# One hybrid decoder layer on Trainium2: attention row maxima passed by a 0/1 matmul, GpSimd scalings a step later, and two norms computed in another place

## The chip, the core and the metric

The kernel runs on one core of a Trainium2 chip: TensorE (PE) multiplies matrices, VectorE (DVE), ScalarE (ACT) and GpSimd (POOL) work on tiles of 128 partitions, SyncE (SP) and the other queues issue DMAs between HBM and SBUF. The metric is the time of one execution in device microseconds; the median of three runs of the kernel before is 1704.49 us (1704.07 to 1704.84).

## What is computed

One step of a decoder layer for a prompt of 512 tokens and 8 samples of 4 tokens each, 544 tokens in all, model width 1024:

```
x += 0.5 * SwiGLU_1(rms(x))                              # width 2816
h  = rms(x); qa, ka, va, qkv_b, z, b, a, gate = split(h @ w_in)
o_a = merge over 3 groups (window, dilation) = (128,1), (512,4), (2048,16)
      of softmax(q k / sqrt(128) - alibi) v              # 4 heads x 128 in each group
o_b = gated DeltaNet: conv of width 4, 8 heads, chunked exact solve, head norm, silu(z)
x += (sig(gA) * (o_a @ w_proj_a) + sig(gB) * (o_b @ w_proj_b)) @ w_out
x += 0.5 * SwiGLU_2(rms(x));   y = rms(x)

def _rms(x, w):  y = x * rsqrt(mean(x * x, -1) + 1e-6);  return y * w
def _merge_groups(outs, lses):  w = softmax(stack(lses), 0);  return sum(w[..., None] * stack(outs), 0)
```

It also returns the new rows of the caches, the convolution states and the DeltaNet states.

## The kernel before

Activations lie transposed, 128 features on the partitions and the 544 tokens as columns, in eight tiles x of 128x544; the columns are worked in two halves of 272 (NH). Weights come from HBM as f32 chunks (raw) and are split into a rounded part and a rest (G): ScalarE copies the rounded part, VectorE or GpSimd subtracts it (`split_next`, line 426). The activations are split in the same way (xh and xl, hh and hl, oh and ol). A unit is one tile of 128 matrix columns for one half: for each of its 128x128 weight tiles three matmuls, hi by xh, hi by xl and lo by xh, into one PSUM bank (`unit`, line 609), and an evacuation by VectorE or ScalarE. All engine instructions are recorded at one helper line, L122, so rows are told apart by their tiles.

`kernel_units` (line 677) walks through all units in a fixed order: feed-forward 1, the mixer, feed-forward 2. Everything else in the mixer is side work in Python generators: `attn_slot` (line 1459, four slots, one for each head of a group), `attn_sample`, `gdn_pair` (line 1056, four pairs of heads), the sample part of the DeltaNet, convolutions, z, `fin_a` (line 854, which brings the slots' outputs into the projection's input). Between two triples of matmuls `pump` (line 643) lets those generators take a step that are ready by the counted costs of the class `Meter` (line 48). Where something must have happened first (a convolution buffer free, SBUF tiles reserved), `until` (line 292) calls `force`, which steps the side work in order of its due time with no unit matmul between, until the condition holds. So the order on TensorE is set when the program is built.

SyncE's queue works in order: an instruction that waits holds up all loads behind it. In `attn_slot` the scores of a slot lie with tokens on the partitions in two layouts (positions of group 0, and of groups 1 and 2); to merge the groups, each layout needs the row maxima of the other (tile ast, X in the code). They are written to a DRAM scratch (md) and read back permuted, two writes and two reads a slot on SyncE's queue. A slot's output o goes to DRAM (oad) and `fin_a` reads it back.

In `gdn_pair` GpSimd scales v and k (tiles vk and kn) of both heads; VectorE makes the decay rows R, ScalarE exponentiates them; then TensorE makes the products of keys and queries (kq), and VectorE scales these into B and A. Later a chain of small steps (X, Pm, Y, Q, called lev in the code) inverts the block matrix: TensorE, then VectorE or ScalarE, then TensorE again.

At the start `build` (line 471) issues eight warm-up passes (WARM=4 f32 matmuls on zeros), splits half 0 of x, adds up the squares of half 0 on GpSimd (`norm_acc`, acc), splits half 1 and adds up its squares; `norm_fin` for half 0 comes after four units: a matmul with ones sums over the partitions, then nine VectorE operations on 128x272 make 1/rms. At the end the same happens for the last half, and `store_y` multiplies its eight tiles by it, two of them on GpSimd, and stores them.

Of the kernel before, what the change touches and what calls it, by code (L numbers as in the profile page):

```python
# [10 lines left out]
F32 = mybir.dt.float32  # L11
# [27 lines left out]

CFG = dict(S=62, S2=4, G=4, G2=8, RAW=2, U3=3, H=10, HM=6, LA=4, LAG=3.0, SLACK=0.0, BANKS=3, PRE=3, LOV=("pa", "pb", "ba", "z", "gate", "gdn", "at"), CV=0, WARM=4, EP=8, DUE=2, RES=0, RQ="gpsimd")  # L40

# [164 lines left out]
def consts():  # L206
# [54 lines left out]
class Builder:  # L261
# [214 lines left out]
    def build(self):  # L476
        nc, A = self.nc, self.A
        self.x = [self.S(name="x") for _ in range(KT)]
        vec = self.C([P, A["in_vec_dram"].shape[1]], name="vec")
        mats = self.C([P, A["in_mats_dram"].shape[1]], name="mats")  # L480
        warm = self.H()
# [19 lines left out]
        for k, n in enumerate(names):  # L501
            setattr(self, n, mats[:, k * P:(k + 1) * P])
        o = len(names) * P
        self.hb, self.mb, self.mh, self.cs = (mats[:, o:o + 32], mats[:, o + 32:o + 40],
                                              mats[:, o + 40:o + 44], mats[:, o + 44:o + 47])
        self.wn = [vec[:, k * 8:(k + 1) * 8] for k in range(4)]
# [3 lines left out]
        self.acc, self.r = [None, None], [None, None]  # L510
# [23 lines left out]
    def norm_acc(self, n, h):  # L534
        s = self.sl(h)
        if n == 0:
            self.acc[h] = [self.S([P, NH], name="acc")]
            self.act(self.acc[h][0], self.x[n][:, s], AF.Square)
        else:
            q = self.H()  # L540
            self.act(q, self.x[n][:, s], AF.Square)
            if self.last and n == KT - 1 and h == 1:
                self.acc[h].append(q)
            else:
                self.tt(self.acc[h][0], self.acc[h][0], q, ALU.add, self.nc.gpsimd)
        if self.last:
            self.act(self.x[n][:, s], self.x[n][:, s], AF.Copy, scale=self.wn[3][:, n:n + 1])
# [32 lines left out]
    def norm_fin(self, h):  # L580

        ps = self.mm_ps()[:, :NH]
        acc = self.acc[h]
# [14 lines left out]
        if h == 1:  # L598
            self.norm_no += 1

    def store_y(self, h):
        s = self.sl(h)
        for n in range(KT):
            f = self.H()
            self.tt(f, self.x[n][:, s], self.R(h), ALU.mult, self.nc.gpsimd if n % 3 == 2 else None)
            (self.nc.scalar if n % 2 and h else self.nc.sync).dma_start(self.A["out_y"][:, n, s], f)
# [70 lines left out]
    def kernel_units(self):  # L677
# [176 lines left out]
    def fin_a(self):  # L854
# [4 lines left out]
        for j in range(4):  # L859
            yield from self.need(3, True)  # L860
            t = self.S([P, NPR], name="oA")
            self.dma(t, self.oad[j])
            yield t
            hl = (self.S(dt=F32R, name="oh"), self.S(dt=F32R, name="ol"))
# [191 lines left out]
    def gdn_pair(self, h0):  # L1056
# [402 lines left out]
    def attn_slot(self, j):  # L1459
# [63 lines left out]
        lay = [lambda a: a.rearrange("s (a p) -> p (s a)", p=P), lambda a: a.rearrange("s (n r) -> n s r", r=4)]  # L1523
        fl = lambda a, i: a.rearrange("p s a -> p (s a)") if i == 0 else a
# [4 lines left out]
        yield X  # L1529
        yield "vector"  # L1530
# [312 lines left out]
```

## Time and profile before

| | us |
|---|---|
| median of three runs | 1704.49 |
| profiled execution | 1707.67 |
| its span, first to last instruction | 1705.8 |
| TensorE busy | 1646.0 (96%) |
| VectorE busy | 1012.1 (59%) |
| ScalarE busy | 620.8 (36%) |
| GpSimd busy | 165.5 (10%) |

The granted TensorE clock is 0.984 in the mean over the span (1 is 2.4 GHz, the upper of its two levels). Busy shares are averages over stages with different limits: feed-forward 1 runs from about 46 to 420 us, the mixer to about 1130, feed-forward 2 to about 1690, and the stages differ in how much of TensorE they use.

### The profile page before, as it was taken

How to read it: one execution, taken by the hardware profiler on the slowest of the kernel's cores; microseconds unless marked ns; L12 is line 12 of the kernel's file. 1: busy time of each engine (PE TensorE's matmuls, PEld its weight loads, DVE VectorE, ACT ScalarE, POOL GpSimd, SP SyncE). 2: the span in 40 equal slices, each digit the busy share in tenths (PEclk: the TensorE clock that was granted, in tenths of full speed). 3: DMA queues.
4: the chain of work that ended last, by engine and by line, in shares of the span. 5: the costliest groups of instructions: out<-in, count | busy, mean ns of one | idle time of the engine just before them, and what ended most of it. 6: DMA issues, size and time to landing. Idle time of an engine off the chain costs nothing.

```text
span 1705.8 us, 33626 instructions
## 1 busy us (share of the span) xinstructions
PE 1646.0 (96%) x13373; PEld 1604.1 (94%) x13373; DVE 1012.1 (59%) x2473; ACT 620.8 (36%) x1559; POOL 165.5 (10%) x289
## 2 busy tenths in 40 slices
PE   8999999999999999989999889899999999999997
PEld 7999999999898999988989779889999999999996
DVE  7754255545777978567785755353456654255534
ACT  5332223333453434445433345432333332232332
POOL 5000000011011211211121110000011000000012
PEclk9999999999999999999999989999999999999999
DMA  5222223221524454656666455432242323222221
GB/s 179 87 88 89 97 76 99 76 86 63 185 76 123 149 172 148 201 149 195 177 184 206 145 183 184 109 118 87 88 138 88 100 75 100 87 85 90 87 76 65
DMA packets 116434, 205.12 MB, mean 120 GB/s; under 512 B 30963, under 2 KB 57109, under 8 KB 116277
## 3 DMA queue, kind: packets, MB, share of 16 engines
q1 hardware_dynamic: 104708, 162.43, 30.4%
q0 software_dynamic: 10992, 39.99, 8.0%
q8 instruction: 105, 1.72, 0.4%
q10 hardware_dynamic: 576, 0.56, 0.1%
q14 instruction: 53, 0.43, 0.1%
HBM read 172.20 MB, written 30.73 MB: 119 GB/s over the span
## 4 chain that ended last, share of the span: by engine, by line
PE 81%; DVE 9%; DMA 5%; ACT 3%; issue 2%; SPq 1%; DVEq 0%; ACTq 0%
PE sd L122 42%; PE mm L122 39%; DMA md<-ast 3%; DVE H L122 1%; DVE G L122 1%; DVE inv L122 1%; DVE y L122 1%; ACT s L122 1%; SPq L122 1%; DMA ast<-md 1%; DVE Yc L122 1%; DVE R L122 1%; DVE nrm L122 1%; DVE xl L122 0%; ACT G L122 0%
## 5 line engine op out<-in xcount | busy, mean ns | idle before, releaser
L122 PE MATMUL mm<-xh,G 128*128 128x272 f32 x3632 | 743.7, 295 | 4.4 <-ACT G L122 2.0
L122 PEld LDWEIGHTS mm<-xh,G 128*128 128x128 f32 x3632 | 591.0, 191 | 18.2 <-issue 10.2
L122 PE MATMUL mm<-xl,G 128*128 128x272 f32 x1816 | 527.2, 290 | 0.4 <-DVE xl L122 0.4
L122 DVE TENSOR_TENSOR G<-raw,G 128x512 fp32r<-128x512 f32 x468 | 303.0, 689 | 169.9 <-ACT G L122 163.8
L122 PE MATMUL sd<-xh,G 128*128 128x272 f32 x1904 | 362.9, 288 | 0.0
L122 PEld LDWEIGHTS mm<-xl,G 128*128 128x128 f32 x1816 | 346.9, 191 | 1.8 <-DVE xl L122 0.6
L122 ACT ACTIVATE G<-raw 128x512 fp32r<-128x512 f32 x474 | 271.9, 622 | 105.4 <-PE mm L122 46.9
L122 PEld LDWEIGHTS sd<-xh,G 128*128 128x128 f32 x1904 | 300.0, 188 | 0.2
L122 PE MATMUL sd<-xl,G 128*128 128x272 f32 x952 | 273.6, 287 | 0.0
L122 PEld LDWEIGHTS sd<-xl,G 128*128 128x128 f32 x952 | 179.1, 188 | 0.1
L122 PE MATMUL sd<-hh,G 128*128 128x272 f32 x1287 | 163.1, 288 | 0.0
L122 PEld LDWEIGHTS sd<-hh,G 128*128 128x128 f32 x1287 | 161.9, 188 | 0.1
L122 POOL TENSOR_TENSOR acc<-acc,H 128x272 f32<-128x272 f32 x55 | 44.8, 815 | 917.6 <-ACT H L122 916.5
L122 ACT ACTIVATE hh<-H 128x272 fp32r<-128x272 f32 x88 | 38.0, 432 | 201.7 <-DVE H L122 201.7
L122 PE MATMUL mm<-hh,G 128*128 128x272 f32 x825 | 104.7, 288 | 0.0
L122 PEld LDWEIGHTS mm<-hh,G 128*128 128x128 f32 x825 | 103.8, 188 | 0.0
L122 ACT ACTIVATE H<-H 128x272 f32<-128x272 f32 (+1 forms) x89 | 38.2, 429 | 162.3 <-DVE H L122 162.3
L122 POOL DMA_DIRECT2D raw<-in_W_dram x76 | 41.5, 546 | 530.4 <-DVE G L122 280.7
L122 DVE SCALAR_TENSOR_TENSOR H<-H,H 128x272 f32<-128x272 f32 x120 | 54.5, 455 | 33.4 <-ACT H L122 32.8
L122 DVE SCALAR_TENSOR_TENSOR x<-sd,x 128x272 f32<-128x272 f32 x49 | 21.4, 438 | 78.2 <-PE sd L122 78.2
L122 DVE SCALAR_TENSOR_TENSOR y<-U,vec,y 128x568 f32<-128x568 f32 x72 | 61.1, 848 | 8.0 <-ACT y L122 5.1
L122 DVE TENSOR_TENSOR hh<-H,hh 128x272 fp32r<-128x272 f32 x88 | 38.9, 442 | 43.9 <-ACT hh L122 43.9
(262 smaller groups left out, 1772.4 us busy)
## 6 DMA issues: line engine op xcount, KB each, us to landing
raw<-in_W_dram SPq DMA_DIRECT2D x161, 512.0 KB, 3.5
raw<-in_W_dram POOLq DMA_DIRECT2D x76, 512.0 KB, 3.9
qkv<-qd SPq DMA_DIRECT2D x36, 256.0 KB, 3.8
st<-in_ssm_dram SPq DMA_DIRECT2D x32, 256.0 KB, 4.6
cache<-in_kc_dram SPq DMA_DIRECT2D x28, 256.0 KB, 4.6
cache<-in_vc_dram SPq DMA_DIRECT2D x28, 256.0 KB, 3.8
qd<-av SPq DMA_DIRECT2D x24, 256.0 KB, 2.7
out_dram<-av SPq DMA_DIRECT2D x24, 256.0 KB, 2.9
```

The lines of the kernel that those rows point to most:

```text
L122: r = f(*args, **kw)
```

## The change

Five things change.
1. `attn_slot`: the maxima go from one layout to the other by TensorE. Each layout's maxima are spread by a 0/1 mask over 32 columns, multiplied by a 0/1 matrix (by4 or its transpose of4, new columns of the constant tile mats), masked again and summed over four. The four DMAs through md go.
2. The last slot (j == 3) keeps its output in SBUF for `fin_a`.
3. `gdn_pair`: the four GpSimd scalings stand after each head's B and A step in place of before the R step.
4. The start: six warm-up matmuls, all first weight splits on VectorE (EP=0), the last two squares of half 0 handed to the norm's matmul in place of GpSimd's adds, `norm_fin(0)` after three units, and the splits and squares of half 1 behind it.
5. The end: `norm_end` makes the last 1/rms with tokens on the partitions, so its chain works on 128x3, and brings it back by a diagonal matrix and matmuls with ones; all eight products are VectorE's.

```diff
-... WARM=4, EP=8, ...
+... WARM=6, EP=0, ...
@@ mats
+    by4 = (blk4[None, :] == (i % 32)[:, None]).astype(np.float32)
+    m4 = ((i % 4)[:, None] == np.arange(4)[None, :]).astype(np.float32)
@@ build
-        seq(xw, 0, {3: (0,), 5: (1,), 7: (0, 1)})
+        seq(xw, 0, {3: (0,), 5: (0,), 7: (0, 0)})
...
-        seq(xw, 1, {})
-        seq(self.norm_acc, 1, {})
+        self.second_half = lambda: (seq(xw, 1, {}), seq(self.norm_acc, 1, {}))
@@ norm_acc
-            if self.last and n == KT - 1 and h == 1:
+            if self.last and n == KT - 1 and h == 1 or self.norm_no == 0 and h == 0 and n >= KT - 2:
                 self.acc[h].append(q)
@@ norm_fin
+        if self.last and h == 1:
+            return self.norm_end(h)
+    def norm_end(self, h):
+        acc, self.acc[h] = self.acc[h], None
+        ps = self.sd_ps()
+        for c, o in enumerate((0, P, NH - P)):
+            for i, a in enumerate(acc):
+                self.mm(ps[:, 4 * c:4 * c + 4], a[:, o:o + P], self.ones[:, 0:4], i == 0, i == len(acc) - 1)
+        v, r, t = (self.T([P, 3], F32, "end", 3) for _ in range(3))
+        self.ts(v, ps[:, 0:12].rearrange("p (c f) -> p c f", f=4)[:, :, 0], 1.0 / DM, EPS, ALU.mult, ALU.add)
+        for _ in self.rsqrt(r, v, t, 2):
+            pass
+        d = self.S([P, 3, P], name="diag")
+        self.tt(d, self.ident.unsqueeze(1).to_broadcast([P, 3, P]), r.unsqueeze(2).to_broadcast([P, 3, P]), ALU.mult)
+        pr = self.sd_ps()
+        self.mm(pr[:, 0:P], self.ones, d[:, 0, :])
...
+        self.store_y(h)
@@ kernel_units
-            if ui in (3, 6):
-                self.norm_fin(ui // 3 - 1)
+            if ui == 2:
+                self.norm_fin(0)
+                self.second_half()
+            elif ui == 6:
+                self.norm_fin(1)
@@ gdn_pair
         for i, h in enumerate(H):
-            self.tt(vk[h], vk[h], bc(ki[:, i * 4:i * 4 + 4]), ALU.mult, pg)
-            self.tt(kn[h], kn[h], bc(c1[:, i * 4:i * 4 + 4]), ALU.mult, pg)
...                                  # B and A of head h
+            self.tt(vk[h], vk[h], bc(ki[:, i * 4:i * 4 + 4]), ALU.mult, pg)
+            self.tt(kn[h], kn[h], bc(c1[:, i * 4:i * 4 + 4]), ALU.mult, pg)
@@ attn_slot
-        md = self.D([2, 2, NPR], "md")
...
-        for i in range(2):
-            self.dma(lay[i](md[i]), fl(X[:, 0, i], i))
-        for i in range(2):
-            self.dma(fl(X[:, 1, i], i), lay[i](md[1 - i]))
+        self.tt(far[0], up(X[:, 0, 0]).rearrange("p s a r -> p s r a"), mk(self.m4).rearrange("p s a r -> p s r a"), ALU.mult)
+        self.tt(far[1], up(X[:, 0, 1]).rearrange("p s r a -> p s a r"), mk(self.mh).rearrange("p s r a -> p s a r"), ALU.mult)
+        yield
+        self.mm(cols(0), self.by4, far[1].rearrange("p s a r -> p (s a r)"))
+        self.mm(cols(1), self.of4, far[0].rearrange("p s r a -> p (s r a)"))
+        yield "vector"
+        for i, m in ((0, self.m4), (1, self.mh)):
+            t = self.T([P, 2, 4, 4], F32, "astf", 4)
+            self.tt(t, cols(i).rearrange("p (s b c) -> p s b c", s=2, b=4), mk(m), ALU.mult)
+            nc.vector.tensor_reduce(X[:, 1, i], t, axis=AX.X, op=ALU.add)
@@ attn_slot's end
-        yield "w"
-        self.dma(self.oad[j], o)
+        if j == 3:
+            self.last_slot = o
...
```

How the change moves instructions is seen in the order of each engine. First TensorE, before, at the evacuation of a convolution unit about a quarter into the mixer: kq is the key and query product of a pair, cache the samples' keys, X, B, Y and Pm the steps of the inversion.

```order
L122 MATMUL sd_7246<-kq_5750 128x256 x2
L122 MATMUL sd_7020<-cache_7007,ex_7013 32x128 x4
L122 MATMUL sd_7020<-cache_7009,ex_7013 32x128 x4
L122 MATMUL sd_7265<-X_7193,B_6126 128x64 x4
L122 MATMUL sd_7265<-X_7197,B_6175 128x64 x4
L122 MATMUL sd_7020<-cache_7011,ex_7013 32x256 x2
L122 MATMUL sd_7280<-kq_5751 128x256 x2
L122 MATMUL sd_7287<-Y_6953,Pm_7194 128x64 x4
L122 MATMUL sd_7287<-Y_6959,Pm_7198 128x64 x4
L122 MATMUL sd_7306<-kq_6291 128x256 x2
L122 MATMUL sd_7313<-X_7193,B_6126 64x64 x4
```

At the same unit, in the kernel after:

```order
L122 MATMUL sd_7341<-X_7320,B_6106 128x64 x4
L122 MATMUL sd_7341<-X_7324,B_6168 128x64 x4
L122 MATMUL sd_7356<-Y_6981,Pm_7321 128x64 x4
L122 MATMUL sd_7356<-Y_6987,Pm_7325 128x64 x4
L122 MATMUL sd_7369<-astf_7353,mats_80 128x32
L122 MATMUL sd_7369<-astf_7352,mats_80 128x32
L122 MATMUL sd_7378<-X_7320,B_6106 64x64 x4
L122 MATMUL sd_7378<-X_7324,B_6168 64x64 x4
L122 MATMUL sd_7397<-Y_6981,Q_7387 64x64 x4
L122 MATMUL sd_7397<-Y_6987,Q_7387 64x64 x4
L122 MATMUL sd_7424<-vk_5642,Y_6981 128x128
L122 MATMUL sd_7424<-vk_5802,Y_6987 128x128
```

The kq rows of that pair now stand earlier; the stretch without unit rows (xh and xl) is 41 groups long in place of 15, and holds levels, a slot (astf, then s and pT) and the samples one after the other.

Second, TensorE at the end of the mixer's side work, before: the last products pT by qkv of the last slot, and the unit behind them.

```order
L122 MATMUL sd_13792<-pT_13772,qkv_13406 128x128
L122 MATMUL sd_13792<-pT_13772,qkv_13408 128x128
L122 MATMUL mm_13779<-xh_4837,G_13607 128x272
L122 MATMUL mm_13779<-xl_4838,G_13607 128x272
L122 MATMUL mm_13779<-xh_4837,G_13607 128x272
L122 MATMUL mm_13779<-xh_4882,G_13607 128x272
L122 MATMUL mm_13779<-xl_4883,G_13607 128x272
```

And after: the last side row of the mixer, os, belongs to the samples.

```order
L122 MATMUL mm_13404<-xh_4747,G_13261 128x272
L122 MATMUL sd_13414<-mats_80,os_13402 128x128 x2
L122 MATMUL mm_13404<-xh_4819,G_13261 128x272
L122 MATMUL mm_13404<-xl_4820,G_13261 128x272
L122 MATMUL mm_13404<-xh_4819,G_13261 128x272
L122 MATMUL mm_13404<-xh_4841,G_13264 128x272
L122 MATMUL mm_13404<-xl_4842,G_13264 128x272
```

Before, 60 unit matmuls lie between the last side row and the first unit of the projections (which reads oh and ol); after, 399.

Third, VectorE at the start, before: xl is the split of half 1, H and r the first operations of the chain for half 0.

```order
L122 SCALAR_TENSOR_TENSOR xl_121<-x_77,vec_79,xh_120 128x272
L122 SCALAR_TENSOR_TENSOR xl_123<-x_78,vec_79,xh_122 128x272
L122 TENSOR_SCALAR vec_79<-vec_79 128x96
L122 TENSOR_SCALAR vec_79<-vec_79 128x1
L122 TENSOR_SCALAR H_359<-sd_357 128x272
L122 TENSOR_SCALAR r_361<-H_359 128x272
L122 TENSOR_SCALAR r_361<-r_361 128x272
```

And after:

```order
L122 TENSOR_SCALAR H_283<-sd_279 128x272
L122 TENSOR_SCALAR r_285<-H_283 128x272
L122 TENSOR_SCALAR r_285<-r_285 128x272
L122 TENSOR_TENSOR H_284<-r_285 128x272
L122 SCALAR_TENSOR_TENSOR H_284<-H_284,H_283 128x272
L122 SCALAR_TENSOR_TENSOR r_285<-H_284,r_285 128x272
L122 TENSOR_TENSOR H_284<-r_285 128x272
L122 SCALAR_TENSOR_TENSOR H_284<-H_284,H_283 128x272
L122 SCALAR_TENSOR_TENSOR r_285<-H_284,r_285 128x272
L122 SCALAR_TENSOR_TENSOR xl_113<-x_71,vec_79,xh_112 128x272
L122 SCALAR_TENSOR_TENSOR xl_115<-x_72,vec_79,xh_114 128x272
```

The chain of half 0 now stands ahead of the splits of half 1; four weight splits G follow them ahead of the first evacuation.

## Rows read from the trace of the kernel before

**Rows 1.** The page: busy time by engine; a costly group (busy us, mean ns).

```profile
PE 1646.0 (96%) x13373; PEld 1604.1 (94%) x13373; DVE 1012.1 (59%) x2473; ACT 620.8 (36%) x1559; POOL 165.5 (10%) x289
...
L122 DVE TENSOR_TENSOR G<-raw,G 128x512 fp32r<-128x512 f32 x468 | 303.0, 689 | 169.9 <-ACT G L122 163.8
```

**Rows 2.** Busy time by stretches: window, length, each engine, PE clock, DMA.

```profile
510.00:536.00 26.00, 22.00 (x150) 21.32 (x149) 17.63 (x51) 9.87 (x29) 6.69 (x10) 0.87 0.43 133
536.00:736.00 200.00, 198.90 (x1775) 189.28 (x1774) 152.98 (x451) 85.35 (x245) 34.89 (x80) 1.00 0.52 161
736.00:760.00 24.00, 18.57 (x165) 16.96 (x162) 10.38 (x29) 10.34 (x33) 3.00 (x6) 0.86 0.57 146
...
940.00:1000.00 60.00, 47.65 (x354) 44.39 (x353) 43.62 (x141) 21.49 (x63) 9.92 (x17) 0.86 0.50 152
...
1075.00:1130.00 55.00, 46.41 (x341) 44.72 (x340) 27.70 (x70) 26.46 (x69) 3.50 (x6) 0.91 0.36 100
1130.00:1690.00 560.00, 560.00 (x4463) 559.51 (x4462) 281.37 (x560) 174.34 (x361) 21.21 (x28) 1.00 0.29 91
```

**Rows 3.** The same view, the 8 us behind the stop at 528.

```profile
527.98:536.00 8.02, 8.02 (x38) 7.56 (x39) 2.87 (x10) 2.07 (x5) 0.57 (x1) 0.65 0.40 133
```

**Rows 4.** Waits of TensorE, 505 to 1130: us in total, times, longest.

```profile
PE sd L122 <- ACT vk L122: 9.1, 1, 9.1
```

**Rows 5.** Timeline 521 to 528: start, us, instruction, [idle before <- releaser].

```profile
521.68 5.32 DVE L122 SCALAR_TENSOR_TENSOR R<-R,gc,mats 128x128 f32<-128x128 f32 x8
521.85 1.08 POOL L122 TENSOR_TENSOR vk<-vk,nrmk 128x512 f32<-128x512 f32 x1 [0.54 <-DVE nrmk L122]
...
524.99 1.08 POOL L122 TENSOR_TENSOR kn<-kn,nrmk 128x512 f32<-128x512 f32 x1
...
527.98 0.90 PE L122 MATMUL sd<-mats,av 128*128 128x128 f32 x3 [4.00 <-ACT av L122]
```

**Rows 6.** Timeline of VectorE, 835: R alone, and a maximum that waits for md.

```profile
835.09 0.17 DVE L122 TENSOR_TENSOR ast<-ast 128x8 f32<-128x8 f32 x1 [3.15 <-DMA ast<-md]
...
835.46 2.19 DVE L122 SCALAR_TENSOR_TENSOR R<-R,gc,mats 128x128 f32<-128x128 f32 x8
```

**Rows 7.** Timeline 719: an operation of VectorE with PSUM input beside GpSimd.

```profile
719.57 1.30 POOL L122 TENSOR_TENSOR zm<-stk,mats 128x512 fp32r<-128x512 f32 x1 [0.20 <-PE sd L122]
719.90 0.41 DVE L122 TENSOR_TENSOR Y<-Y,sd 128x256 f32<-128x256 f32 x1
```

**Rows 8.** Timeline 735 to 755: SyncE's queue, and TensorE.

```profile
735.92 2.34 SPq L122 DMA_DIRECT2D md<-ast  x2
750.06 0.98 SPq L122 DMA_DIRECT2D ast<-md  x2
...
754.03 0.66 PE L122 MATMUL sd<-cache,ex 128*32 128x64 f32 x16 [5.43 <-DMA cache<-in_kc_dram]
```

**Rows 9.** Timeline 608: a step of the inversion on TensorE and VectorE.

```profile
608.17 2.00 PE L122 MATMUL sd<-X,B 128*128 128x64 f32 x16
...
611.34 0.74 DVE L122 TENSOR_TENSOR Pm<-sd,mats 128x256 f32<-128x256 f32 x2
```

**Rows 10.** Timeline of the start: GpSimd, VectorE and TensorE.

```profile
13.83 7.67 POOL L122 TENSOR_TENSOR acc<-acc,H 128x272 f32<-128x272 f32 x7
17.98 7.05 DVE L122 SCALAR_TENSOR_TENSOR xl<-x,vec,xh 128x272 fp32r<-128x272 f32 x8
...
23.51 0.62 PE L122 MATMUL sd<-acc,mats 128*128 128x272 f32 x2
...
28.55 1.42 DVE L122 SCALAR_TENSOR_TENSOR H<-H,H 128x272 f32<-128x272 f32 x1
...
35.46 1.24 PE L122 MATMUL mm<-acc,mats 128*128 128x272 f32 x2 [2.36 <-DVE H L122]
```

**Rows 11.** Timeline of the end: VectorE.

```profile
1694.64 0.44 DVE L122 TENSOR_SCALAR H<-mm 128x272 f32<-128x272 f32 x1 [1.40 <-PE mm L122]
...
1698.71 3.35 DVE L122 TENSOR_TENSOR H<-x,r 128x272 f32<-128x272 f32 x6
```

More of the change, by code (lines that the diff above doesn't have):

```diff
@@ L38 @@
 NORMED = (8, 9)
-CFG = dict(S=62, S2=4, G=4, G2=8, RAW=2, U3=3, H=10, HM=6, LA=4, LAG=3.0, SLACK=0.0, BANKS=3, PRE=3, LOV=("pa", "pb", "ba", "z", "gate", "gdn", "at"), CV=0, WARM=4, EP=8, DUE=2, RES=0, RQ="gpsimd")
+CFG = dict(S=62, S2=4, G=4, G2=8, RAW=2, U3=3, H=10, HM=6, LA=4, LAG=3.0, SLACK=0.0, BANKS=3, PRE=3, LOV=("pa", "pb", "ba", "z", "gate", "gdn", "at"), CV=0, WARM=6, EP=0, DUE=2, RES=0, RQ="gpsimd")
 MIX_ORDER = [("a", 0), ("p", 0), ("p", 1), ("p", 2), ("a", 1), ("p", 3), ("a", 2), ("a", 3), ("p", 4), ("a", 4), ("p", 5), ("a", 5)]
@@ L240, in consts @@
     cs = np.array([[SLOPES[4 * g + r // 32] / SCALE for g in range(3)] for r in row], np.float32)
-    mats = np.concatenate([ident, tri, negm, tri_s, neg_s, ones_s, m1, one, hb, mb, mh, cs], 1)
+    by4 = (blk4[None, :] == (i % 32)[:, None]).astype(np.float32)
+    m4 = ((i % 4)[:, None] == np.arange(4)[None, :]).astype(np.float32)
+    mats = np.concatenate([ident, tri, negm, tri_s, neg_s, ones_s, m1, one, hb, mb, mh, cs, by4, by4.T, m4], 1)
     at = np.concatenate(t0 + [t1, t2, ts], 1)
@@ L480, in build @@
         mats = self.C([P, A["in_mats_dram"].shape[1]], name="mats")
+        self.ones = self.C([P, P], name="ones")
+        nc.gpsimd.memset(self.ones, 1.0)
         warm = self.H()
@@ L500, in build @@
         names = ["ident", "tri", "negm", "tri_s", "neg_s", "ones_s", "m1", "ones"]
-        for k, n in enumerate(names):
+        for k, n in enumerate(names[:-1]):
             setattr(self, n, mats[:, k * P:(k + 1) * P])
@@ L505, in build @@
                                               mats[:, o + 40:o + 44], mats[:, o + 44:o + 47])
+        o += 47
+        self.by4, self.of4, self.m4 = mats[:, o:o + P], mats[:, o + P:o + 2 * P], mats[:, o + 2 * P:o + 2 * P + 4]
         self.wn = [vec[:, k * 8:(k + 1) * 8] for k in range(4)]
@@ L509, in build @@
         self.gn = vec[:, 196:197]
-        self.acc, self.r = [None, None], [None, None]
+        self.acc, self.r, self.norm_no = [None, None], [None, None], 0
         self.xn = [(self.S(dt=F32R, name="xh"), self.S(dt=F32R, name="xl")) for _ in range(KT)]
@@ L599, in norm_fin @@
             self.norm_no += 1
+    def norm_end(self, h):
[12 more added lines that the diff above has]
+        self.mm(pr[:, 0:P], self.ones, d[:, 0, :])
+        self.mm(pr[:, P:2 * P], self.ones, d[:, 1, :])
+        self.mm(pr[:, 2 * P:NH], self.ones, d[:, 2, 3 * P - NH:])
+        self.r[h] = pr[:, :NH]
+        self.store_y(h)
     def store_y(self, h):
@@ L604, in store_y @@
             f = self.H()
-            self.tt(f, self.x[n][:, s], self.R(h), ALU.mult, self.nc.gpsimd if n % 3 == 2 else None)
+            self.tt(f, self.x[n][:, s], self.R(h), ALU.mult, self.nc.gpsimd if n % 3 == 2 and h == 0 else None)
             (self.nc.scalar if n % 2 and h else self.nc.sync).dma_start(self.A["out_y"][:, n, s], f)
@@ L683, in kernel_units @@
         self.xn2, self.normed = [], [False, False]
-        self.use, self.norm_no = [False, False], 0
+        self.use = [False, False]
         for ui, u in enumerate(self.units):
@@ L859, in fin_a @@
         for j in range(4):
[L860 to L863, printed above, removed]
+            if j == 3:
+                yield from self.need(2, True)
+                t, self.last_slot = self.last_slot, None
+            else:
+                yield from self.need(3, True)
+                t = self.S([P, NPR], name="oA")
+                self.dma(t, self.oad[j])
+                yield t
             hl = (self.S(dt=F32R, name="oh"), self.S(dt=F32R, name="ol"))
@@ L1520, in attn_slot @@
                 self.act(s[:, e, :], s[:, e, :], AF.Exp, scale=SCALE, bias=m, accum_out=den)
-        yield "w"
-        md = self.D([2, 2, NPR], "md")
-        lay = [lambda a: a.rearrange("s (a p) -> p (s a)", p=P), lambda a: a.rearrange("s (n r) -> n s r", r=4)]
-        fl = lambda a, i: a.rearrange("p s a -> p (s a)") if i == 0 else a
-        for i in range(2):
-            self.dma(lay[i](md[i]), fl(X[:, 0, i], i))
-        for i in range(2):
-            self.dma(fl(X[:, 1, i], i), lay[i](md[1 - i]))
-        yield X
+        yield "vector"
+        far = [self.T([P, 2, 4, 4], F32, "astf", 4) for _ in range(2)]
+        up = lambda a: a.unsqueeze(3).to_broadcast([P, 2, 4, 4])
+        mk = lambda a: a.unsqueeze(1).unsqueeze(1).to_broadcast([P, 2, 4, 4])
+        self.tt(far[0], up(X[:, 0, 0]).rearrange("p s a r -> p s r a"), mk(self.m4).rearrange("p s a r -> p s r a"), ALU.mult)
+        self.tt(far[1], up(X[:, 0, 1]).rearrange("p s r a -> p s a r"), mk(self.mh).rearrange("p s r a -> p s a r"), ALU.mult)
+        yield
+        px = self.sd_ps()
+        cols = lambda i: px[:, 32 * i:32 * i + 32]
+        self.mm(cols(0), self.by4, far[1].rearrange("p s a r -> p (s a r)"))
+        self.mm(cols(1), self.of4, far[0].rearrange("p s r a -> p (s r a)"))
+        yield "vector"
+        for i, m in ((0, self.m4), (1, self.mh)):
+            t = self.T([P, 2, 4, 4], F32, "astf", 4)
+            self.tt(t, cols(i).rearrange("p (s b c) -> p s b c", s=2, b=4), mk(m), ALU.mult)
+            nc.vector.tensor_reduce(X[:, 1, i], t, axis=AX.X, op=ALU.add)
         yield "vector"
@@ L1579, in attn_slot @@
         self.tt(ov, ov, po.rearrange("p (r n) -> p r n", r=4), ALU.add)
-        yield "w"
-        self.dma(self.oad[j], o)
-        self.free(9)
+        if j == 3:
+            self.last_slot = o
+            self.free(8)
+        else:
+            yield "w"
+            self.dma(self.oad[j], o)
+            self.free(9)
         self.slots_done += 1
```

## The prediction

> **What bounds the kernel now.** I read the busy line first: TensorE is busy for 1646.0 us of a span of 1705.8 [rows 1], so all its idle time is 59.8 us, and nothing but idle or slow TensorE time can be won. The view by stretches comes second, with the granted clock beside the busy time. The two feed-forward blocks are full at clock 1.00; what is missing lies in a few stretches of the mixer and at both ends [rows 2]. An idle stretch also costs afterwards: in the 8.02 us behind one stop TensorE is always busy, yet the granted clock is 0.65 [rows 3], a mix of the levels 2.4 and 1.2 GHz, so about 0.35 x 8.02 = 2.8 us are lost on top of the stop. For a stretch I therefore count its length less the busy time, plus the busy time multiplied by (1 - clock). By rows 2:
> 510 to 536: 4.00 + 22.00 x 0.13 = 6.9.
> 736 to 760: 5.43 + 18.57 x 0.14 = 8.0.
> 940 to 1000: 12.35 + 47.65 x 0.14 = 19.0.
> 1075 to 1130: 8.59 + 46.41 x 0.09 = 12.8.
> These four sum to 46.7 us, 2.7% of the span; between 536 and 736 almost nothing is missing (198.90 of 200 busy). The list of waits comes third: its longest entry, 9.1 us, is in the third of the stretches [rows 4].
>
> **The scalings in GpSimd.** Before 528 the eight decay rows R take VectorE 5.32 us while GpSimd runs four scalings of 1.08 us (the first at 521.85, the last at 524.99). ScalarE's exponentials wait for R, and behind them stands the copy av, for which TensorE waits 4.00 us [rows 5]. The same eight without GpSimd beside them take 2.19 [rows 6]. The change puts the scalings behind the B and A steps; the R step is 3.13 us shorter, and the order now has the two matmul groups of kq ahead of the av ones, so the stop and the slow time behind it go. I take 6.6 of the 6.9. The scalings themselves stay, now beside operations of which one input is in PSUM. Row: one such operation, Y, took 0.41 us in the middle of a GpSimd product of 1.30 [rows 7], against 0.42 for the like operations elsewhere, so I charge B and A nothing. If that cover failed it would be a doubling of 16 operations of 0.34, that is 5 us of VectorE for a pair, none of it on TensorE's path as long as side work is not late. For whatever VectorE work the 16 scalings now meet instead (17 us in all) I charge 1.0; the bounds are 0 and, if all of them delayed TensorE, 17.
> The Trainium skill (SBUF — State Buffer, "SBUF: two separate sides") says that VectorE and GpSimd share one port pair as an exclusive lock, taken by a VectorE operation with two SBUF inputs against a GpSimd operation that reads SBUF, and that the loser waits fully. The trace agrees in the R step, which stretches from 2.19 to 5.32, and in Y, which does not. [...]
>
> **The row maxima without DRAM.** Each slot wrote its row maxima out and read them back in another layout: SyncE's queue issues the writes at 735.92 and the reads only at 750.06, because they wait for the writes; the cache loads stand behind them in that queue, and TensorE waits 5.43 us for one at 754.03 [rows 8]. Four DMAs a slot go, and with them this wait: I take the whole 8.0. What is added: two mask products, two matmuls of 128x32, two products and two reductions a slot. A VectorE operation on 8 columns takes 0.17 [rows 6]; the wider ones (32 columns) I put at 0.25, so eight with their hand-overs are 2 us of VectorE, off the path. The matmuls are TensorE time for good: between 0.1 and 0.3 us each (the 16 of 64 columns take 2.00 together [rows 9]), with the mask's weight load; four slots make 1.2 us.
>
> **What the planner makes of it.** The side work is laid between unit matmuls by a planner that counts costs, so each removed wait moves it. The order shows three things.
> First, a new stretch without units, at the place where before 15 side groups filled each other: now 41 side groups stand there in a row, with no unit matmul between, because an evacuation waits for a free convolution buffer. Many are a chain TensorE, VectorE, TensorE: from X,B (608.17 + 2.00) over the two products Pm at 611.34 to the next use of them is 1.9 us [rows 9]. The 41 groups hold some 24 us of TensorE work by the lengths of their counterparts; three chains (levels, one slot, the samples) run beside each other, so I take the longest, some 32 us. That is 8 us idle, and 2 more for the clock: 10. Bounds: 6, if the chains fill each other as before, and 18, if the clock falls for the whole stretch.
> Second, a stretch of 16 such groups later, where before the 940 to 1000 stretch lay (its wait of 9.1 us for vk [rows 4] is of the same kind). I count 8 for it, 3 for the thick side work behind it and 3 for one more short one: 14 in place of 19.0, so 5.0 saved (between -3 and +10).
> Third, all side work ends much sooner. Before, the last two slots end 60 unit matmuls ahead of the first projection, and the projection's inputs are late. Now 399 unit matmuls lie between, at 0.125 us each (4463 in 560 us [rows 2]) some 50 us. The 12.8 us of 1075 to 1130 go, but 1.0 that I leave: 11.8.
>
> **The start.** GpSimd's seven adds took 7.67 us from 13.83 [rows 10]; five end at about 13.83 + 5 x 1.10 = 19.3, so the norm's matmul can end at 20.6, not 24.1 as at 23.51 + 0.62. The nine operations of the chain then run beside GpSimd's adds of half two. One took 1.42 beside GpSimd work, against 0.44 alone [rows 10, 11]; the split xl beside adds 0.88 (7.05 for 8). At 0.8 in the mean they end at 27.8. Then come eight xl (0.47 each, 31.6) and four splits G at 0.69 [rows 1], which GpSimd no longer does; the first evacuation stands at 34.5, about where it was. But unit 4 needs the first xl of half two, 28.3, and the units before it end at about 23.6 even with the gain of 2 us from the longer warm-up: 4.7 us idle in place of the 2.36 and 0.6 at 35.46 [rows 10]. Put together I make it 1.0 us longer, between -1.5 and +2.5.
>
> **The end.** Nine operations of the chain on 272 columns (0.44 for the first, 1694.64, and 4.07 us from there to the products at 1698.71 [rows 11]) become nine on three columns (about 0.2 with the hand-over, from the 0.17 of rows 6), 2.2 us less; then a diagonal product (0.5), three matmuls (0.7) and two hand-overs, and the eight products all on VectorE (0.56 each beside GpSimd's two, 3.35 for six [rows 11], and 0.47 alone: 3.8, so 0.4 more). With 0.4 for the hand-overs the sum is -2.2 + 0.5 + 0.7 + 0.4 + 0.4 = -0.2, between -0.7 and +0.5. The tile of ones and the last slot's output kept in the chip's memory cost nothing that TensorE waits for.
>
> **The sum.** -6.6 - 8.0 - 5.0 - 11.8 + 10 + 1.0 + 1.2 + 1.0 - 0.2 = -18.4 us. The profiled execution took 1707.67 us with 1.9 around its span, so 1689.3 for its counterpart; it stands 3.2 above the median of 1704.49, which gives 1686.1.
>
> **Rivals.**
> A. The new stretches without units are dear. If each of the 57 groups cost a full hand-over not filled by another chain, from 608.17 + 2.00 to the next dependent matmul, about 1.6 us, they would cost 91 us, not 24. That the gap is not filled at all is excluded by the three chains; at 1.0 each they cost 57, so the time is 1686 + 33 = 1719. Slower than before begins at 0.8 a group, which is half the hand-over. For it: before 1000 one such stretch had 9.1 us of idle in a single wait [rows 4]. Against it: the 15 groups from 606 on stand in the stretch of 200 us that lost only 1.1 [rows 2].
> B. What was late stays late. The tail is ready 50 us sooner in the order, but if its chain (row maxima, softmax, projection inputs) ends by DMA and VectorE rather than by TensorE's order, the 11.8 stay: 1698.
> C. No change: the first pair and the maxima gain 14.6, the stretches cost 24 rather than 10 net, and the tail gives half: within 3 us of 1704.
> D. The new stretches fill themselves as the 15 groups did: 10 + 14 becomes 12, so 1674.
> E. The step does nothing, since the scalings still meet the R step: excluded, the order has them behind both heads' R.
>
> **How the numbers follow.** Forecast (1679 to 1694) 0.50, D 0.13, B 0.17, C 0.08, A 0.12. A measurement of this kernel tells about 0.2% (3.4 us) from no change. Faster: 0.50 + 0.13 + 0.17 = 0.80; same 0.08; slower 0.12. The range 1674 to 1702 leaves out A, most of C and a third of D: 0.8 inside.
>
> **What would show it.** In the profile after: no stop at 528 and R at 2.2 for eight; no wait for a cache load behind the maxima; about 600 to 640 a stretch of small matmuls whose busy time is near 24 of 32 us; a tail into the projections with clock 1.00; the first evacuation near 34.5 with a TensorE stop of 4 to 5 us near 24. A busy time below 16 us in that stretch, or a second one of the same size at 950, would make the prediction wrong on the slow side; a full 1075 to 1130 with stretches that lose under 12, on the fast side.

## The result and the profile after

The kernel after takes 1695.25 us (median of four, 1693.2 to 1696.35), the kernel before 1704.66 beside it: ratio 0.9942, interval 0.9928 to 0.9955, 9.4 us or 0.55% less. The interval lies clear of 1: it is faster, with half of the forecast gain of 18.4. The profiled execution of after took 1696.35 us with a span of 1694.6, so the two profiled executions differ by 11.3 us, and that difference is the one taken apart below.

The busy line of the page after, against [rows 1]:

```profile
PE 1653.0 (98%) x13411; PEld 1611.4 (95%) x13411; DVE 1006.5 (59%) x2506; ACT 622.6 (37%) x1559; POOL 152.8 (9%) x280
```

TensorE's idle time fell from 59.8 to 41.6 us, by 18.2. But its busy time rose by 7.0: it was busy longer with nearly the same work. The view by stretches of after says where (window, length, busy time of each engine, TensorE's clock, DMA):

```profile
511.00:537.00 26.00, 25.76 (x195) 24.99 (x194) 20.95 (x65) 12.10 (x34) 4.83 (x10) 1.00 0.46 137
606.00:612.00 6.00, 3.58 (x27) 3.39 (x26) 5.61 (x12) 4.04 (x15) 1.27 (x3) 0.90 0.33 87
612.00:630.00 18.00, 16.09 (x102) 14.06 (x101) 8.56 (x34) 3.45 (x14) 3.85 (x8) 0.50 0.57 187
630.00:648.00 18.00, 15.98 (x149) 13.97 (x146) 14.23 (x47) 7.10 (x19) 2.01 (x7) 0.87 0.03 12
736.00:764.00 28.00, 25.20 (x174) 23.13 (x173) 21.30 (x73) 13.87 (x36) 8.36 (x18) 0.95 0.67 212
784.00:796.00 12.00, 9.09 (x56) 7.38 (x53) 9.74 (x28) 7.63 (x26) 1.11 (x2) 0.86 0.92 296
966.00:984.00 18.00, 14.39 (x139) 12.57 (x131) 13.03 (x47) 6.23 (x17) 4.17 (x5) 0.81 0.76 259
1075.00:1120.00 45.00, 45.00 (x360) 45.00 (x359) 14.98 (x29) 16.44 (x38) 3.71 (x7) 1.00 0.31 94
```

The first row answers to 510 to 536 in [rows 2]: the stop is gone. The last answers to 1075 to 1130: TensorE is full up to the projections and beyond. The second to fourth are the new stretch of side work without units; from 537 to 606, ahead of it, TensorE is never idle. In its middle, 18 us long, TensorE is busy for 16.09 us, a share that a reader may take for good, but at clock 0.50, the lower level throughout: half of that busy time is lost, 8.05 us. The stretch loses (6.00 - 3.58 + 0.36) + (1.91 + 8.05) + (2.02 + 2.08) = 16.8 us.

The waits of TensorE after, from 505 to 1120 (us in total, times, longest), to be set against [rows 4] and the stop in [rows 8]:

```profile
PE sd L122 <- DVE Pm L122: 3.4, 2, 2.8
PE sd L122 <- DVE X L122: 2.9, 2, 2.4
PE sd L122 <- ACT vk L122: 2.8, 1, 2.8
PE sd L122 <- DVE astf L122: 2.4, 2, 1.5
```

No wait for a cache load is left, and none for a maximum in DRAM. The wait for vk is 2.8 in place of 9.1. What is new is small: astf, the masked maxima, 2.4 us in two waits, and steps of the inversion (X, Pm).

VectorE and GpSimd after, where the stop was and at two later pairs (start, us, instruction), against [rows 5, 6]:

```profile
523.19 2.19 DVE L122 SCALAR_TENSOR_TENSOR R<-R,gc,mats 128x128 f32<-128x128 f32 x8
...
528.15 0.34 DVE L122 SCALAR_TENSOR_TENSOR B<-sd,nrmk,R 128x128 f32<-128x128 f32 x1
...
529.07 1.05 POOL L122 TENSOR_TENSOR vk<-vk,nrmk 128x512 f32<-128x512 f32 x1
529.20 1.97 DVE L122 COPY U<-convout 128x24 f32<-128x24 f32 x1
530.08 1.04 POOL L122 TENSOR_TENSOR kn<-kn,nrmk 128x512 f32<-128x512 f32 x1
...
763.35 1.04 POOL L122 TENSOR_TENSOR vk<-vk,nrmk 128x512 f32<-128x512 f32 x1
763.43 0.33 DVE L122 SCALAR_TENSOR_TENSOR B<-sd,nrmk,R 128x128 f32<-128x128 f32 x1
...
865.26 1.05 POOL L122 TENSOR_TENSOR vk<-vk,nrmk 128x512 f32<-128x512 f32 x1
865.31 4.00 DVE L122 SCALAR_TENSOR_TENSOR R<-R,gc,mats 128x128 f32<-128x128 f32 x8
```

GpSimd's two scalings of the first head now run from 529.07 to 531.12. R takes the 2.19 of a quiet GpSimd. B and A take 0.34 at the first pair, where they hardly meet a scaling, and 0.33 at 763.43, in the middle of one. A copy of 128x24 that falls among the scalings takes 1.97 us; in the kernel before the 24 copies of this form take 0.173 in the mean. The last pair is otherwise: GpSimd comes to the first scaling at 865.26, ahead of that pair's first B at 869.67, and R, which starts at 865.31, takes 4.00. The place of the scalings in the program does not hold GpSimd back until VectorE has made B and A.

The start and the end after, against [rows 10, 11], first the start on VectorE and TensorE:

```profile
21.08 0.44 DVE L122 TENSOR_SCALAR H<-sd 128x272 f32<-128x272 f32 x1 [1.60 <-PE sd L122]
21.55 0.83 DVE L122 TENSOR_SCALAR r<-H 128x272 int32<-128x272 int32 x1
...
28.28 3.38 DVE L122 SCALAR_TENSOR_TENSOR xl<-x,vec,xh 128x272 fp32r<-128x272 f32 x8
28.83 0.60 PE L122 MATMUL sd<-xl,G 128*128 128x272 f32 x1 [4.68 <-DVE xl L122]
...
33.99 0.43 DVE L122 TENSOR_TENSOR H<-mm,r 128x272 f32<-128x272 f32 x1
```

The two-input operations of this chain take 0.88 to 0.96 each beside GpSimd's adds. The operation r at 21.55, with one input in SBUF, takes 0.83; its like at the end of the kernel before, with GpSimd quiet, takes 0.30:

```profile
1695.12 0.30 DVE L122 TENSOR_SCALAR r<-H 128x272 int32<-128x272 int32 x1
```

So operations with one SBUF input are stretched as well. Now the end on VectorE after:

```profile
1681.38 0.44 DVE L122 SCALAR_TENSOR_TENSOR x<-mm,x 128x272 f32<-128x272 f32 x1 [3.71 <-PE mm L122]
1683.70 0.16 DVE L122 TENSOR_SCALAR end<-sd 128x3 f32<-128x3 f32 x1 [1.88 <-PE sd L122]
...
1687.65 2.87 DVE L122 TENSOR_TENSOR H<-x,sd 128x272 f32<-128x272 f32 x8 [1.62 <-PE sd L122]
```

The first products of the end stand 6.27 us behind the last residual (1687.65 - 1681.38); before they stood 5.91 behind it (1698.71 - 1692.80). The small chain is short, 1.8 us, but the way there and back by matmuls costs 0.4 more than it gives, and the products, 2.87 for eight on VectorE in place of 3.35 for six beside GpSimd's two, give back 0.5.

### The profile page after: what moved, and what is told of

It reads as the page before. It is cut to its first block, busy times and chain, and to the rows that moved or that the text cites. A ratio compares the mean times of both kernels' runs of the same rounds, so it can differ in the third digit from the quotient of the medians.

```text
span 1694.6 us, 33678 instructions
## 1 busy us (share of the span) xinstructions
PE 1653.0 (98%) x13411; PEld 1611.4 (95%) x13411; DVE 1006.5 (59%) x2506; ACT 622.6 (37%) x1559; POOL 152.8 (9%) x280
## 4 chain that ended last, share of the span: by engine, by line
PE 84%; DVE 9%; ACT 2%; issue 2%; DMA 1%; SPq 1%; POOL 0%; DVEq 0%; ACTq 0%; POOLq 0%
PE sd L122 44%; PE mm L122 40%; DVE y L122 2%; DVE G L122 1%; DVE H L122 1%; ACT s L122 1%; SPq L122 1%; DVE ast L122 1%; DVE kq L122 1%; DVE R L122 0%; DMA raw<-in_W_dram 0%; ACT G L122 0%; DVE nrm L122 0%; DVE r L122 0%; ACT y L122 0%
## 5 line engine op out<-in xcount | busy, mean ns | idle before, releaser
L122 PE MATMUL mm<-xh,G 128*128 128x272 f32 x3632 | 733.3, 293 | 2.9 <-DVE G L122 1.6
L122 PEld LDWEIGHTS mm<-xh,G 128*128 128x128 f32 x3632 | 583.3, 189 | 16.4 <-issue 10.7
L122 DVE TENSOR_TENSOR G<-raw,G 128x512 fp32r<-128x512 f32 x474 | 306.6, 689 | 184.4 <-ACT G L122 180.0
```

What stands on the lines that cost most here:

```text
L122: r = f(*args, **kw)
```

## The experiments

Eleven kernels ran, each timed in five rounds beside the kernel before. A row is a row in the order; "lost" is idle time plus busy time by (1 - clock), summed over windows of 4 us from 420 us to the end of the mixer, as in the prediction. It is 55.1 us before and 40.3 after. By rows, the stretch at 608 of after, 41 groups in the prediction, counts 62.

**1. The scalings put back** (a_no_sc).

```diff
+            self.tt(vk[h], ..., pg); self.tt(kn[h], ..., pg)      # ahead of the R step
             self.stt(R[h][:, c, :], ...)
...
-            self.tt(vk[h], ..., pg); self.tt(kn[h], ..., pg)      # behind B and A
```

> The kernel after with the GpSimd scalings put back ahead of the R step; all else as after. In its order TensorE has no stretch of side matmuls longer than 21 rows (after: one of 62 rows at 608 us). Theory 1 (the move of the scalings removes the stop at 528 but lets the planner lay the 62-row stretch, which costs 16.6 us by idle and clock): the stop of about 6.8 us comes back, the stretch goes, two shorter ones of 21 and 14 rows cost some 6 more than those of after: net -4, about 1691 us. Rival (the stretch is only other people's waiting gathered in one place and costs nothing of its own): only the stop comes back, +6.8, about 1702 us.

It took 1701.36 us (ratio 0.9973, 0.9962 to 0.9984), some 5 more than after. Its stretches:

```profile
524.00:536.00 12.00, 8.13 (x41) 7.46 (x40) 6.06 (x15) 3.64 (x8) 3.00 (x4) 0.72 0.27 95
606.00:650.00 44.00, 43.91 (x400) 40.28 (x399) 36.32 (x104) 16.58 (x46) 5.04 (x15) 1.00 0.49 155
930.00:956.00 26.00, 19.41 (x146) 17.23 (x147) 19.98 (x51) 4.36 (x14) 4.61 (x5) 0.67 0.46 151
960.00:976.00 16.00, 10.46 (x56) 9.02 (x55) 14.14 (x45) 5.85 (x19) 4.54 (x6) 0.79 0.38 98
986.00:1000.00 14.00, 11.52 (x71) 10.53 (x69) 8.52 (x25) 7.28 (x20) 4.16 (x10) 0.76 0.76 226
```

Two of the three terms of theory 1 came out: the stop is back (3.87 + 8.13 x 0.28 = 6.1 us) and 606 to 650 lost nothing. The third did not: the later rows lost 13.0 + 7.7 + 5.2 = 25.9 us, where after's pieces lose 15.8 and 6 more than those had been expected. So the time was near the rival's, for another reason than the rival's: the stretch does cost 16 us, but without it dependent work of the same kind (steps of the inversion and the state products behind them) loses more at other places than it does in after.

**2. The scalings alone** (b_sc), the kernel before with the same two lines moved behind B and A.

> The kernel before with the GpSimd scalings moved behind B and A and nothing else. Its order has a 57-row stretch without unit matmuls at the same unit, and a tail of 189 unit matmuls. Theory 1: -6.8 for the stop, +16 for the stretch, about -8 for the tail's late inputs: within 4 us of 1704.7. Rival (the stretch costs nothing): -6.8 - 8, about 1690 us.

Both were wrong: 1720.02 us, ratio 1.008 (1.0066 to 1.0093), 13.6 slower than before. The waits of TensorE, then the rows of SyncE's queue:

```profile
PE sd L122 <- DVE s L122: 27.5, 2, 23.8
```

```profile
1009.17 2.34 SPq L122 DMA_DIRECT2D md<-ast  x2
1017.91 0.98 SPq L122 DMA_DIRECT2D ast<-md  x2
```

In this order TensorE has nothing else at about 1001 us and stands for 23.8 us until a slot's scores come, nearly 13 of them from the write of the maxima to VectorE's first use of what came back (1009.17 to 1021.90). The stretch at 608 cost 15.8. The scalings' move takes 6.4 us off at 528 (6.8 to 0.4), and by the order that follows it lays bare the way through DRAM.

**3. The maxima through DRAM, all else after** (a_no_md); the part of `attn_slot` is that of before.

> The kernel after with the row maxima again through DRAM; all else as after. Its order has a 57-row stretch and a later one of 21, as the run b_sc. Theory 3 (such an order exposes the way through DRAM): it behaves as b_sc did, with TensorE waiting 15 to 30 us for scores or loads in the later stretch: 1715 to 1722. Rival (the maxima are worth only the 7.8 us that the trace of before shows): about 1703.

It took 1719.81 us (1.0082, 1.0068 to 1.0095), as theory 3 had it:

```profile
PE sd L122 <- DVE s L122: 27.3, 2, 23.3
```

The masks and small matmuls are thus worth 24 us in this order, three times the wait that the trace of before showed, and without them the whole change would have been a loss.

**4. The head of the stretch filled** (a_fill).

```diff
+                if self.ui == 174:
+                    for _ in range(20):
+                        self.nc.tensor.eng.matmul(self.bank[:, NH:512], hi, xh[:, 0:512 - NH], start=True, stop=True)
                 self.until(lambda: self.convs[1] - self.convs[0] < 2 + CFG["CV"])
```

> The kernel after with 20 matmuls of 240 columns more, into unused columns of a PSUM bank, at the head of the stretch at 608 us, where TensorE is idle for 2.42 us waiting for X; the rest of the order is unchanged. Theory 2a (the idle of 2.4 us brings the clock down and the thin side work keeps it down): with the gap filled the clock stays at 1.00 through the stretch and about 8 us go: about 1687 us. Theory 2b (the small side matmuls by themselves bring it down): the clock falls a few us later all the same, and at most 2 us go: about 1694 us.

It took 1692.65 us (0.9922, 0.991 to 0.9935), about 3 less than after by the ratios, with intervals that overlap. Its rows from 608 on:

```profile
608.00:612.00 4.00, 3.65 (x32) 3.34 (x30) 2.37 (x5) 3.97 (x16) 2.62 (x5) 1.00 0.72 190
612.00:616.00 4.00, 3.07 (x26) 2.99 (x27) 2.57 (x8) 0.00 (x0) 2.45 (x6) 0.89 1.02 380
616.00:620.00 4.00, 3.26 (x29) 2.88 (x27) 1.10 (x8) 0.81 (x2) 0.00 (x0) 0.50 0.98 372
620.00:624.00 4.00, 3.55 (x20) 2.92 (x20) 3.76 (x14) 0.38 (x1) 0.00 (x0) 0.50 0.03 13
624.00:628.00 4.00, 4.00 (x35) 1.95 (x34) 3.90 (x14) 2.00 (x7) 0.20 (x1) 0.83 0.01 4
```

The gap is filled, and the clock falls all the same, at 615 in place of 611; in the 4 us in which it falls TensorE is idle for 0.93 us in all. It is back at 625, not 631. So 2a fails, and 2b is right that the clock comes down in thin side work without a long gap (0.59 us at the longest). Whether the gap has a part in how long it stays down, 10 us here against 20, is not shown: in experiment 10 the gap is there, in the same order, and the clock is down for 13.

**5. Another order, by one constant** (a_lag32). `pump` lets a step start when VectorE's and ScalarE's counted time is less than LAG ahead of TensorE's.

```diff
-... LAG=3.0, ...
+... LAG=3.2, ...
```

> The kernel after with one planner constant changed, LAG from 3.0 to 3.2, which lays the same side work in another order: its longest stretch without unit matmuls is 13 rows, and 219 unit matmuls lie behind the last side row. Theory 1 (the stretches are what the change lost): some 16 us less at 608 and 5 less later, a few more in the small ones: about 1680 us (1676 to 1687). Rival (what is lost follows the side work wherever it is laid): within 3 us of 1695.

It took 1668.95 us, ratio 0.9783 (0.977 to 0.9797): 37 us less than before, 26 less than after, and 7 below the range of theory 1. The mixer in its profile:

```profile
420.00:500.00 80.00, 75.94 (x588) 74.72 (x588) 61.78 (x160) 36.85 (x92) 8.51 (x25) 0.98 0.41 132
500.00:700.00 200.00, 199.48 (x1754) 191.24 (x1752) 153.69 (x482) 87.98 (x265) 34.55 (x78) 1.00 0.49 155
700.00:900.00 200.00, 195.07 (x1732) 182.62 (x1730) 155.66 (x490) 91.80 (x298) 38.58 (x73) 1.00 0.57 180
900.00:1093.00 193.00, 187.94 (x1642) 176.63 (x1639) 115.58 (x350) 88.93 (x251) 24.64 (x43) 1.00 0.55 179
```

The lost time is 15.9 us, 24.4 less than after, and of it only 1.3 by the clock (after: 18.3). The same operations laid between units, 13 side rows at most in a run, cost little.

**6 to 8. The constant without the change, and a third value** (b_lag32, b_lag35: before; a_lag35: after).

> The kernel before with LAG 3.2 in place of 3.0, nothing else. Its order has one stretch of 38 rows without unit matmuls and a tail of 150. Theory 3 (what is lost is set by where the order puts the dependent side work; the change only takes away waits that such an order can expose: the scalings beside R, the maxima through DRAM): the stop at 528 of 6.8 us stays, the stretch costs about 12, the maxima some 8 or more: 1692 to 1706 us, and the same constant with the change (1669) is over 20 us faster. Rival (LAG 3.2 is worth 26 us by itself and the change little): about 1680 us.

> The kernel before with LAG 3.5. No stretch longer than 17 rows, a tail of 54. Theory 3: the stop at 528, the maxima and the late inputs of the projections stay (27 us together before), the stretches cost little: about 1697 us (1690 to 1706). Rival (the stretches are all that counts): about 1680 us.

> The kernel after with LAG 3.5. It has again a stretch of 53 rows at the same unit as after, a later one of 24, and a tail of 354. Theory 3: the 53 rows cost about 15 us as after's 62 do, no stop at 528, no wait for maxima: 1690 to 1697 us. Rival (LAG above 3.0 is what helps): about 1670 us.

| LAG | before | lost | after | lost | after less before |
|---|---|---|---|---|---|
| 3.0 | 1 | 55.1 | 0.9942 (0.9928 to 0.9955) | 40.3 | -0.6% |
| 3.2 | 0.9946 (0.9934 to 0.9958) | 50.0 | 0.9783 (0.977 to 0.9797) | 15.9 | -1.6% |
| 3.5 | 1.0092 (1.0068 to 1.0117) | 67.0 | 0.9966 (0.9953 to 0.9979) | 45.2 | -1.3% |

b_lag32 (1696.27 us) fell into theory 3's range; the rival had it at 1680. b_lag35 (1718.49 us) was 12 above the top of the range: short stretches in the order did not make it good, since its losses lie in many small waits (TensorE waits 7.6 us in four for r, 5.9 for av behind the decay rows, 3.7 for scores, and some 12 us are lost by late inputs again from 1108 to 1140). a_lag35 (1699.54) lies 2.5 above its range; the 53 rows, 30.3 us long, cost 3.90 + 6.07 = 10.0 us, less than said, and 980 to 1012 cost 9.83 + 6.21 = 16.0, which had not been expected. The rows, and the longest wait of TensorE in the second of them:

```profile
610.10:640.40 30.30, 26.40 (x228) 22.67 (x228) 20.64 (x70) 11.60 (x38) 5.82 (x14) 0.77 0.41 129
980.00:1012.00 32.00, 22.17 (x118) 19.61 (x117) 23.44 (x70) 7.83 (x26) 7.83 (x15) 0.72 0.56 172
PE sd L122 <- DMA qkv<-qd: 5.0, 1, 5.0
```

The later place, with far fewer side rows in a run (24 at most by the order), lost more than the 53, and 5.0 of it in one wait for a DMA: the count of rows alone does not set the price.

In each order the change gains, by 9, 28 and 21 us; and a step of the constant moves the time by as much as the change does.

**9. A long stretch late** (a_lag315), the kernel after with LAG=3.15.

> The kernel after with LAG 3.15. Its order has no stretch at 608 us but one of 39 and one of 61 rows late in the mixer, and 540 unit matmuls behind the last side row. Theory 1 (long stretches without units cost about 0.27 us a row, 62 rows 16.6): 100 rows cost 26, the rest as in a_lag32: about 1694 (1690 to 1700). Rival (only the stretch at 608 is dear, or a LAG near 3.2 helps by itself): 1670 to 1675.

It took 1700.58 us (0.9975, 0.9965 to 0.9985), just above the range of theory 1 and 26 from the rival. At 608 nothing is lost, late in the mixer much is:

```profile
604.50:613.60 9.10, 9.10 (x78) 6.98 (x78) 5.80 (x19) 0.59 (x1) 6.22 (x11) 1.00 0.38 116
927.50:953.20 25.70, 17.21 (x132) 13.34 (x132) 19.37 (x68) 7.31 (x25) 7.26 (x13) 0.80 0.59 190
953.20:974.00 20.80, 14.71 (x97) 14.11 (x97) 13.14 (x52) 9.04 (x27) 1.74 (x4) 0.78 0.46 134
988.80:1014.50 25.70, 19.98 (x169) 17.04 (x168) 18.00 (x55) 11.69 (x41) 0.73 (x2) 0.87 0.37 133
```

The first, second and fourth rows are runs without a unit matmul, of 12, 39 and 61 rows. The short one loses nothing, the long ones 8.49 + 3.44 and 5.72 + 2.60, 20.3 us together, for which 26 had been expected. Between them, where units and waits for the inversion alternate, another 6.09 + 3.24 = 9.3 are lost, which theory 1 did not have.

**10. Start and end as before** (a_no_start_end), the mixer as after.

```diff
-... WARM=6, EP=0, ...
+... WARM=4, EP=8, ...
...                                  # first splits and norm_fin(0) as before
-        if self.last and h == 1:
-            return self.norm_end(h)
```

> The kernel after with the start (warm-up, first splits, first 1/rms) and the end (last 1/rms) as before; the order of the mixer is that of after. Read from the profiles of before and after, the start lost 1.0 us and the end 0.2: 1.2 us less than after, about 1694 us. Rival (the changed start or end gives something that is spent later): 1 to 2 us more than after.

1691.39 us, ratio 0.9919 (0.9907 to 0.9931): 3.9 less than after, not 1.2, though the intervals just overlap. Set side by side by unit matmuls, the profile shows 1.01 us less behind the start, 0.8 still at 590 us, and then 4.7 less at unit matmul 4800, behind the stretch at 608: there the clock was low from 612.9 to 626.3, and in after from 611.0 to 631.3 and again from 642 to 645. The two rows, this kernel's and that of after:

```profile
612.90:626.30 13.40, 12.05 (x72) 10.81 (x72) 7.14 (x28) 1.19 (x3) 2.05 (x6) 0.50 0.62 223
```

```profile
611.00:631.30 20.30, 18.19 (x108) 15.83 (x108) 10.44 (x40) 4.93 (x19) 5.06 (x11) 0.50 0.55 178
```

The order is the same in both, so I do not put that part down to the start.

**11. LAG 3.2 with start and end as before** (a_lag32_ns), to tell this apart.

> The kernel after with LAG 3.2, and with the start and the end as before; the mixer's order is that of the run a_lag32. By the profiles the new start costs 0.9 to 1.0 us and the new end 0.2, and there is no long stretch in which the clock can fall: 1.2 us less than a_lag32 (1669.0), about 1667.7. Rival (the 3.9 us that the start and the end were worth in a_no_start_end are theirs, not those of a clock that came back earlier in the stretch): about 1665.

1668.26 us, 0.7 below a_lag32, with the same ratio of 0.9783 (0.977 to 0.9797). With no long stretch the 3.9 us are not there, so the rival falls; 1.2 us are less than such medians can tell. This kernel and a_lag32 are the fastest of the study, 37 us under the kernel before.

## Why the prediction was right, and where it was off

It forecast faster with 0.80, and 1695.25 lies in the range of 1674 to 1702; but the likeliest time, 1686, was 9 us too low. By its own terms, with the lost time by windows of 4 us:

| step | predicted | measured |
|---|---|---|
| the stop at 528 | -6.6 | -6.8 (6.8 to 0) |
| the wait for maxima and cache, 748 to 760 | -8.0 | -7.8 (7.8 to 0) |
| the new stretch at 606 to 648 | +10 | +16.6 |
| 940 to 1000, and what takes its place | -5.0 | -1.6 (17.4 to 15.8) |
| the tail, 1075 to 1130 | -11.8 | -12.7 (12.7 to 0) |
| small stops elsewhere in the mixer | 0 | -3.2 (10.2 to 7.0) |
| TensorE's own new work | +1.2 | +2.5 |
| what the moved scalings meet | +1.0 | in the rows above |
| the start | +1.0 | +0.9 |
| the end | -0.2 | +0.2 |

The measured terms add up to -11.9; the remaining 0.6 to the 11.3 of the two profiles is in stops under 0.3 us and in rounding. The 3.2 us of small stops were not forecast; that they make up for about half of what the new stretch cost beyond its 10 is luck.

**What held.** Three steps that were read straight from rows of before came out within 1 us, and so did the start, in its details too: the norm's matmul was put to end at 20.6 and the chain at 27.8, and the chain ran from 21.08 to 28.36, the first xl at 28.3 (28.28), the first evacuation at 34.5 (33.99), TensorE's new stop at 4.7 us (4.68). Rival E was excluded by the order of the program; that held where it counted, at the first pair, but not at the last, where R took 4.00 us beside a scaling (TensorE, busy for 7.79 of the 8 us from 864, can have lost 0.2 there at most). D did not come; B, that what was late stays late, lay near in time (1698) but not in its mechanism, since 1075 to 1120 is full.

**The step that was mis-sized** is the first of "what the planner makes of it": "That is 8 us idle, and 2 more for the clock: 10." The idle time was 6.3 us. The clock cost 10.3, five times what I took, since I counted the low time as in [rows 3], as a few us behind one stop, where dense units follow. Here thin side work follows, small matmuls with hand-overs between, and the clock stayed at 0.50 for 20 us with TensorE 90% busy (18.19 of 20.30 from 611.0 to 631.3). The bound of 18 "if the clock falls for the whole stretch" was the nearer case, though the clock was low for some 23 of the 38 us. Experiment 4 shows that the clock falls in the thin work without the first gap too; experiments 5 and 9 that the loss at 608 goes where no long stretch lies there, and that one laid elsewhere loses too, 8.3 to 11.9 us.

The second term, 14 for the later stretch, measured 15.8 in pieces (756 to 764, 784 to 796, 968 to 984), near enough; what was off was the 19.0 it was set against. The mean clock of a wide window also counts idle time, in which a low clock costs nothing (from 980 to 984 before, TensorE is idle for all 4.00 us at a mean of 0.59); summed over windows of 4 us the stretch of before had lost 17.4. The matmuls of astf take 0.63 us a slot at the upper clock (1.01 at the lower) rather than 0.3, 2.5 in all.

**The cover of the moved scalings** held as said for B and A. What they meet instead is, at the first pair, a copy of 24 columns that takes 1.97 us, off TensorE's path there. Later they meet sums of the convolution (three y in 4.49 and in 4.62, where three take 2.49 at 769.25), two products kq (3.91 for 0.75) and the last R. That is some 11 us more of VectorE, within the bounds of 0 and 17, but in the windows of 4 us where this happens TensorE was busy for 31.8 of 32 us at clock 1.00, so the 1.0 does not show there; whether a later wait stems from it is not shown. In the kernel before, the scalings cost VectorE some 14 us, at the worst a product of 0.3 us that took 4.44, until four scalings were done:

```profile
879.52 4.44 DVE L122 TENSOR_TENSOR inv<-Yc,Uc 128x128 f32<-128x128 f32 x1
```

So the move did not end the conflict of the two engines; it took it off the place where TensorE waited for it. The Trainium skill (SBUF — State Buffer, "SBUF: two separate sides") counts plain copies among the operations of VectorE that take the shared port pair in a fast mode; the row of that copy agrees, 1.97 against 0.173, and the prediction had weighed only operations with two inputs.

**What it did not see** is that the parts are not independent. The prediction priced each by the waits in the trace of before. Experiments 1 to 3 show other prices: the scalings alone cost 13.6 us, with the maxima in place they give about 5; the maxima are worth 24 us with the scalings moved, against 7.8 in the trace of before. The reason is seen in the rows of b_sc: each part changes the order that the planner lays, and what an order exposes is not what the old one did.

**What stays open.** Why the clock was low for 20 us in one kernel and for 13 in another of the same order isn't told by these runs, nor whether this makes the spread of after's four executions. Nor is it shown why LAG 3.2 and not 3.15 or 3.5 gives the good order.

## What to carry to other kernels

Where a planner sets the order from counted costs, a change's price is not the sum of the waits it removes: build the new order first, look for runs of dependent side work without dense work between, follow the waits in each (a DMA in it can cost more than many rows), and price a good part of a long one at the lower clock level, not a few us behind the first gap: here 20 of 38 us, and 13 in another kernel of the same order. A share of 90% busy proves nothing without the granted clock beside it. An instruction that stands later in the program on another engine is not thereby later in time: look up where it ran. And before a few tenths of a per cent are put down to an edit, move a constant that only reshuffles the order: here it moved the time by as much as the change, and in the best order the change was worth three times what it showed at first.

## What the runs showed of the hardware

TensorE's clock stayed at the lower of its two levels for 20 us while the engine was 90% busy with small matmuls (611.0 to 631.3 after), and in the filled stretch (experiment 4) it fell in the 4 us from 612, in which TensorE was idle for 0.93 us in all, with no gap over 0.6. A copy of 128x24 on VectorE took 1.97 us in place of 0.17 beside GpSimd's products, and a product of 128x128 took 4.44 in place of 0.3 until four of them in a row were done, while operations with an input in PSUM ran in the middle of such a product unchanged, at 0.33 us. Operations with one input in SBUF (r, 128x272) took 0.83 in place of 0.30 beside GpSimd's adds.
